# A two-layer decoder trunk on one core: the last row tile in three pieces, one weight split on VectorE, and two steps of the first mixer in another order

## The chip, the core and the metric

The kernel runs on one core of a Trainium2 chip. A core has a matrix engine (TensorE, PE in the profile; PEld is its loading of weights), a vector engine (VectorE, DVE), an engine for activation functions (ScalarE, ACT), GpSimd (POOL) and SyncE (SP), which here only issues DMA transfers. Each engine works through its own instructions in order and waits on semaphores for the others. Matrix products are written to PSUM, which has eight banks of 128 x 512 floats; all other tiles lie in SBUF.

The metric is the time of one execution on the device in microseconds. The kernel before takes 986.98 us, the median of three runs (986.97 to 987.2).

## The reference, cut to what matters

The input has 512 tokens of 1024 features. Two layers follow each other, and each is a mixer and a gated FFN, both with a residual and an RMS norm ahead; a final RMS norm ends it. All is float32.

```python
def forward(x):                       # x: 512 x 1024
    h = x
    # layer 0, even: one input projection, short gated convolution and causal pooling
    proj = rms_norm(h, norm_mix[0]) @ w_in_even          # 1024 -> 2048: b, c, v, z
    y_a = b * causal_dwconv3(c * v, conv_a)
    y_b = einsum(pool(z) - z, w_pool) * pool_scale       # windows 2, 4, 8, 16
    h = h + concat(y_a, y_b) @ w_out_even
    h = h + ffn(rms_norm(h, norm_ffn[0]), 0)
    # layer 1, odd: chunked spatial gating
    u, v = split(gelu(rms_norm(h, norm_mix[1]) @ w_in_odd))
    h = h + (u * spatial(rms_norm(v, sgu_norm))) @ w_out_odd
    h = h + ffn(rms_norm(h, norm_ffn[1]), 1)
    return rms_norm(h, final_norm)

def ffn(x, l):                        # 1024 -> 2816 -> 1024
    g = causal_dwconv3(x @ w_gate[l], conv[l]) + b[l]
    return (silu(g) * (x @ w_up[l])) @ w_down[l]
```

## The kernel before

**Products.** Each float32 operand is held as two parts of a reduced float format: `hi`, a rounded copy, and `lo`, what is left, `x - hi`. A product of two such operands is three matmuls into one PSUM bank (`mm3`, L132 to L135): hi with hi (L133), then the two mixed ones (L134, L135). Making the parts of a weight is two steps. `parts` (L125) rounds on ACT (L128) and subtracts on DVE (L129). `summed` (L116) needs no DVE: ACT writes the negated raw value (L120), a DMA issued by POOL adds it up in flight (L121), and ACT rounds `hi` (L122). Raw weights are loaded by SP into four buffers (`raw`, L109); a load starts when the last reader of its buffer is done, and SP issues its loads in order.

**Order.** The code is written against a tile framework, which places the instructions on each engine and adds the semaphores; calls wrapped in `inorder` keep their order as written. Each engine then runs its list in order, so an instruction that waits holds all that stand behind it on that engine.

**Start, `mixer0` (L333).** The input is loaded in pieces of one or two column blocks together with the matching rows of the z weight. `turn(k)` (L355) transposes block k of the input on PE into a PSUM bank (`xt_ps`, L358), rounds the weight on ACT (L366), copies the block to `h[k]` on DVE (L367), makes the scaled parts `hgh` on ACT (L369) and `hgl` on DVE (L371) from `h[k]`, the low weight part on DVE (L370), and the square for the norm on ACT. `group` (L137) runs the products: block k of the contraction against four column groups, and `ahead` (L377) calls `turn` one block before it is used (blocks 0 and 1 together). Behind the z group the weights of the pooling projection (`wpl`, L426 to L431) are loaded by SP and split, `wpl_hi` on ACT (L430) and `wpl_lo` on DVE (L431). This split stands in neither order as written, and in the built lists it comes between blocks 3 and 4 of z on DVE and on ACT. The norm's scale is applied later: `rstd_tokens` sums the squares on PE (L197, L198), and its root on ACT (L227) and four steps on DVE follow.

**FFN, `Ffn.both` (L651).** Hidden features go in pairs f, f + 1 of 128. For most pairs gate and up are computed by seven products in place of eight on halves of the operands: `s12`, `s34` and so on are sums of raw weight blocks on DVE (L668 to L675), each split into parts (L648, L649). The lower half of the raw weights (`raws[key, 1]`) is split by `summed` (L676), except in the last pair. PE runs 14 products of 12 matmuls (L639). ACT copies results out (L698) and DVE adds others onto them (L703, L708). In layer 1 the pair f = 4 is followed by the down projection of features 0 and 1 (`dn`, 48 matmuls), then by f = 6, and then by f = 8 in `seven` (L726), whose first sums on DVE, called s14 and s23, stand at L746 to L748.

**End, `ffn1` (L1123).** The last down projection takes four hidden blocks (18 to 21) for four row tiles of 128 tokens and two halves of 512 columns: eight groups of 12 matmuls, in `group8` (L1293), row tile by row tile. `done` (L1263) follows each group: DVE adds the product onto the residual `y` (L1266), ACT squares it and sums the squares along the row (L1271), DVE multiplies by the final norm's gain (L1275). After the second half the mean of squares (L1281) goes to `newton` (L223): the root on ACT (L227), its reciprocal on DVE (L228), and one Newton step (L229, L230, L1284), and DVE scales both halves (L1287), which SP stores (L1289).

Of the kernel before, what the change touches and what calls it, by code (L numbers as in the profile page):

```python
# [8 lines left out]
F32 = mybir.dt.float32  # L9
# [3 lines left out]
ALU = mybir.AluOpType  # L13
# [17 lines left out]
def tile_trunk(ctx: ExitStack, tc: tile.TileContext, x, norm_mix, norm_ffn, final_norm,  # L31
# [104 lines left out]

    def group(name, outs, ks, lhs, rhs, tail, on_done, before=None, at_end=None):  # L137
# [172 lines left out]

    def in_group(name, w, c0, lhs_is_weight, on_done, tail, chunks=None, before=None):
        if chunks is None:
# [15 lines left out]
        if lhs_is_weight:  # L328
            group(name, range(4), list(range(NK)), wt, lambda k, j: hg_k(k), tail, on_done, before)
        else:  # L330
            group(name, range(4), list(range(NK)), tokens, wt_wide, tail, on_done, before)

    def mixer0():  # L333
        nonlocal prm0
        w = w_in_even[0]
        with tc.tile_pool(name="m0", bufs=1) as mp:
# [18 lines left out]
            def turn(k):  # L355
# [3 lines left out]
                if k in raws:  # L359
# [5 lines left out]
                whi, wlo, wraw = zchunks[k]  # L365
                inorder(nc.scalar.activation(whi, wraw, AF.Copy))  # L366
                inorder(nc.vector.tensor_copy(h[k], ps))  # L367
                g = prm_mix("mix", k)
                inorder(nc.scalar.activation(hg[k][0], h[k], AF.Copy, scale=g))  # L369
                inorder(nc.vector.tensor_tensor(wlo, wraw, whi.bitcast(F32), ALU.subtract))  # L370
                inorder(nc.vector.scalar_tensor_tensor(  # L371
                    hg[k][1], h[k], g, hg[k][0].bitcast(F32), op0=ALU.mult, op1=ALU.subtract))
                norm.square(k, inorder)
                if k == 0:
                    load(6, 2)

            def ahead(k):  # L377
                for i in (0, 1) if k == 0 else (k + 1,):
                    if i < NK:
                        turn(i)  # L380

# [40 lines left out]

            in_group("z", w, 1536, True, z_done, 2, zchunks, ahead)
            prm0 = params0()
# [4 lines left out]
            wpl_lo = mp.tile([P, 4, P], F32R, name="wpl_lo")  # L429
            nc.scalar.activation(wpl_hi, wpl, AF.Copy)  # L430
            nc.vector.tensor_tensor(wpl_lo, wpl, wpl_hi.bitcast(F32), ALU.subtract)  # L431

# [9 lines left out]

            in_group("ac", w, 512, True, c_done, 4)

            cv = {}
# [43 lines left out]
    class Ffn:  # L489
# [161 lines left out]
        def both(self, f):  # L651
# [12 lines left out]
            for key in "gu":  # L664
# [458 lines left out]
    def ffn1(norm):  # L1123
        with tc.tile_pool(name="f1", bufs=1) as ap:
# [7 lines left out]
            y = [y_all[:, t, :] for t in range(NT)]  # L1132
            ssf = ap.tile([P, NT, PAD], F32, name="ssf")[:, :, :2]

# [7 lines left out]
            def before(i, j):  # L1142
                if i < 2:
                    turn_residual(j, i)

            def minus(dst, x, y_):
# [10 lines left out]
            def down(a):  # L1157
# [74 lines left out]
                yield  # L1232

            for groups, a, b in (((0, 2, 4), 0, 2), ((6, 8), 2, 6), ((10, 12), 6, 10),
                                 ((14, 16), 10, 14), ((18, 20), 14, 18), ((), 18, 22)):
# [16 lines left out]

                def lhs(ft, j):
                    ts_ = slice((j // 2) * P, (j // 2 + 1) * P)
                    return acts[ft][0][:, ts_], acts[ft][1][:, ts_]

                def rhs(ft, j):
                    c = slice((j % 2) * 512, (j % 2 + 1) * 512)
                    return ch[ft][0][:, 0, c], ch[ft][1][:, 0, c]

                yf = {}

                def done(j, ps):  # L1263
                    t, half = j // 2, j % 2
                    dst = y[t][:, half * 512 : (half + 1) * 512]
                    nc.vector.tensor_tensor(dst, ps, dst, ALU.add)  # L1266
                    if not last:
                        return
                    sq = tp.tile([P, S], F32, tag="sq", name=f"sqf{j}")
                    ss = ssf[:, t, half : half + 1]  # L1270
                    nc.scalar.activation(sq, dst, AF.Square, accum_out=ss)  # L1271
                    if half == 0:
                        yf["pair"] = ap.tile([P, 2, S], F32, tag="s", bufs=4, name=f"yf{j}")
                    yf[half] = yf["pair"][:, half, :]
                    nc.vector.tensor_tensor(yf[half], dst, fin[:, half * 512 : (half + 1) * 512],  # L1275
                                            ALU.mult)
                    if half == 0:
                        nc.vector.tensor_scalar(ss, ss, 1.0 / D, EPS, op0=ALU.mult, op1=ALU.add)
                        return
                    ms = ssf[:, t, 0:1]  # L1280
                    nc.vector.scalar_tensor_tensor(ms, ss, 1.0 / D, ms, op0=ALU.mult, op1=ALU.add)  # L1281
                    r = tp.tile([P, LINE], F32, tag="rc", name=f"rc_fin{t}")[:, :1]
                    newton(ms, 1, f"fin{t}", r)
                    nc.vector.tensor_scalar(ms, ms, 1.5, None, op0=ALU.add)  # L1284
                    for c in range(2):
                        cs = slice(c * 512, (c + 1) * 512)
                        nc.vector.tensor_scalar(y[t][:, cs], yf[c], r, ms,  # L1287
                                                op0=ALU.mult, op1=ALU.mult)
                        nc.sync.dma_start(out[t * P : (t + 1) * P, cs], y[t][:, cs])  # L1289

                group8(f"dn{a}", list(range(a, b)), lhs, rhs, 4, done)

    def group8(name, ks, lhs, rhs, tail, on_done):  # L1293
        banks = {}
        head = max(0, len(ks) - tail)
        order = [(i, j) for i in range(head) for j in range(8)]
        order += [(i, j) for j in range(8) for i in range(head, len(ks))]
        for i, j in order:
            if j not in banks:
                banks[j] = mm_bank(f"{name}_{j}") if j < 7 else aux_bank(f"{name}_{j}")  # L1300
            mm3(banks[j], lhs(ks[i], j), rhs(ks[i], j), i == 0, i == len(ks) - 1, inorder)
            if i == len(ks) - 1:
                on_done(j, banks[j])

# [34 lines left out]
```

## Time and profile before

| | |
|---|---|
| median of 3 runs | 986.98 us (986.97 to 987.2) |
| profiled execution | 988.01 us |
| its span, first to last instruction | 986.2 us |
| mean granted TensorE clock | 0.997 |
| busy PE, DVE, ACT, POOL | 973.6, 776.0, 549.5, 61.6 us |
| DMA moved, mean | 126.62 MB, 128 GB/s |

The page gives busy time of each engine over the whole span; it can't say what a stage waits for. For that the trace is asked by stretch: the timeline lists instructions with their start, their duration and, in brackets, the idle time of the engine just before them and what ended it. A row of SPq or POOLq is the issue of a DMA, not its transfer. In the chain of waits the pieces that led to the last instruction stand in order of time.

### The profile page before, as it was taken

What the parts mean: (1) busy time and instruction counts of PE and PEld (TensorE: products, weight loads), DVE (VectorE), ACT (ScalarE), POOL (GpSimd) and SP (SyncE); (2) the same over time, 40 slices, a digit from 0 to 9 for tenths busy, and PEclk for the clock granted to TensorE, in tenths of its full rate; (3) what the DMA queues carried; (4) which work ended last, traced back from release to release, by engine and by line L of the source; (5) the groups of instructions that cost most, each with busy time, mean ns of one, the idle gap of its engine ahead of it and who ended that gap; (6) DMA issues with size and microseconds to landing.
All of it is one profiled execution on the core that took longest, in us unless ns stands there. A gap on an engine that the chain in (4) does not pass through costs nothing.

```text
span 986.2 us, 14472 instructions
## 1 busy us (share of the span) xinstructions
PE 973.6 (99%) x5619; PEld 857.2 (87%) x5619; DVE 776.0 (79%) x1184; ACT 549.5 (56%) x805; POOL 61.6 (6%) x90
## 2 busy tenths in 40 slices
PE   8999999999999999999999999999999999999996
PEld 6888888898999989999888888888898989989885
DVE  6977457968776687768998686489799989898996
ACT  5623346744654646545658844568466567565752
POOL 0032000100000000000000000001000001000000
PEclk9999999999999999999999999999999999999998
DMA  6522225454445544545313412334545646556432
GB/s 227 194 104 87 87 86 128 107 150 129 108 149 149 139 140 107 151 117 195 134 57 119 150 64 87 105 99 109 137 149 153 159 138 150 149 151 171 129 86 86
DMA packets 84784, 126.62 MB, mean 128 GB/s; under 512 B 4356, under 2 KB 53740, under 8 KB 84716
## 3 DMA queue, kind: packets, MB, share of 16 engines
q1 hardware_dynamic: 76172, 100.01, 30.8%
q0 software_dynamic: 7200, 24.12, 13.1%
q10 hardware_dynamic: 1344, 1.58, 0.5%
q8 instruction: 44, 0.72, 0.3%
q14 instruction: 24, 0.20, 0.1%
HBM read 99.47 MB, written 2.10 MB: 103 GB/s over the span
## 4 chain that ended last, share of the span: by engine, by line
PE 93%; DMA 2%; DVE 2%; ACT 1%; issue 0%; SPq 0%; DVEq 0%; ACTq 0%; POOL 0%; POOLq 0%
PE d L134 4%; PE d L133 4%; PE d L135 4%; PE gu L133 2%; PE gu L135 2%; PE gu L134 2%; PE va L934 2%; PE u L133 1%; PE g L133 1%; PE oo L133 1%; PE g L134 1%; PE oo L135 1%; PE u L135 1%; PE oo L134 1%; PE g L135 1%; PE oe L134 1%
## 5 line engine op out<-in xcount | busy, mean ns | idle before, releaser
L134 PE MATMUL d<-a_lo,whi_d 128*128 128x512 f32 x176 | 68.6, 390 | 0.0
L135 PE MATMUL d<-a_hi,wlo_d 128*128 128x512 f32 x176 | 68.5, 389 | 0.0
L133 PE MATMUL d<-a_hi,whi_d 128*128 128x512 f32 x176 | 66.9, 390 | 0.0
L509 DVE SCALAR_TENSOR_TENSOR c<-rows,prm,c 128x512 f32<-128x512 f32 x88 | 64.4, 747 | 2.8 <-ACT c L507 2.8
L121 POOL DMA_DIRECT2D wlo_g<-raw_g x17 | 14.8, 871 | 414.8 <-ACT wlo_g L120 390.7
L292 DVE TENSOR_TENSOR h<-d,h 128x512 f32<-128x512 f32 x48 | 32.6, 688 | 9.4 <-PE d L135 9.3
L129 DVE TENSOR_TENSOR wlo_d<-raw_d,whi_d 128x1024 fp32r<-128x1024 f32 x22 | 26.8, 1224 | 16.5 <-ACT whi_d L128 16.5
L134 PEld LDWEIGHTS d<-a_lo,whi_d 128*128 128x128 f32 x176 | 33.0, 188 | 7.3 <-DVE a_lo L249 0.2
L133 PEld LDWEIGHTS d<-a_hi,whi_d 128*128 128x128 f32 x176 | 32.8, 188 | 7.1
L135 PEld LDWEIGHTS d<-a_hi,wlo_d 128*128 128x128 f32 x176 | 33.0, 188 | 6.8
L520 ACT ACTIVATE s<-c,prm 128x512 f32<-128x512 f32 x44 | 31.3, 717 | 12.3 <-DVE c L509 12.1
L648 ACT ACTIVATE whi_s12u<-s12u 128x1024 fp32r<-128x1024 f32 x14 | 14.8, 1059 | 39.2 <-PE d L134 33.7
L175 ACT ACTIVATE hgh<-h,prm 128x512 fp32r<-128x512 f32 x24 | 17.3, 721 | 28.4 <-DVE h L292 28.4
L648 ACT ACTIVATE whi_s12g<-s12g 128x1024 fp32r<-128x1024 f32 x14 | 14.9, 1061 | 30.6 <-DVE s12g L669 25.0
L507 ACT ACTIVATE c<-rows,prm 128x512 f32<-128x512 f32 x44 | 31.4, 719 | 1.0 <-DVE rows L703 0.4
L128 ACT ACTIVATE whi_d<-raw_d 128x1024 fp32r<-128x1024 f32 x22 | 23.2, 1056 | 14.3 <-issue 3.3
L129 DVE TENSOR_TENSOR wlo_u<-raw_u,whi_u 128x1024 fp32r<-128x1024 f32 x17 | 20.7, 1222 | 11.4 <-ACT whi_u L128 11.4
L176 DVE SCALAR_TENSOR_TENSOR hgl<-h,prm,hgh 128x512 fp32r<-128x512 f32 x24 | 17.9, 750 | 11.8 <-ACT hgh L175 11.8
L121 POOL DMA_DIRECT2D wlo_u<-raw_u x17 | 14.6, 862 | 194.9 <-ACT wlo_u L120 88.4
L133 PE MATMUL gu<-hgh,whi_u 128*128 128x512 f32 x64 | 25.4, 397 | 0.0
L133 PE MATMUL gu<-hgh,whi_g 128*128 128x512 f32 x64 | 25.4, 396 | 0.0
L133 PE MATMUL oo<-mx,whi_oo 128*128 128x512 f32 x64 | 25.2, 394 | 0.0
(1413 smaller groups left out, 3614.4 us busy)
## 6 DMA issues: line engine op xcount, KB each, us to landing
raw_g<-in_w_ffn_gate_dram SPq DMA_DIRECT2D x36, 512.0 KB, 4.0
raw_u<-in_w_ffn_up_dram SPq DMA_DIRECT2D x36, 512.0 KB, 3.7
raw_d<-in_w_ffn_down_dram SPq DMA_DIRECT2D x22, 512.0 KB, 3.7
raw_dn<-in_w_ffn_down_dram SPq DMA_DIRECT2D x22, 512.0 KB, 4.1
wlo_g<-raw_g POOLq DMA_DIRECT2D x17, 512.0 KB, 4.5
wlo_u<-raw_u POOLq DMA_DIRECT2D x17, 512.0 KB, 4.6
raw_oe<-in_w_out_even_dram SPq DMA_DIRECT2D x8, 512.0 KB, 3.5
raw_g<-in_w_ffn_gate_dram SPq DMA_DIRECT2D x16, 256.0 KB, 2.9
```

What stands on the lines that cost most here:

```text
L121: nc.gpsimd.dma_start(lo, raw, accum_op=ALU.add)
L128: nc.scalar.activation(hi, raw, AF.Copy)
L129: nc.vector.tensor_tensor(lo, raw, hi.bitcast(F32), ALU.subtract)
L133: order(nc.tensor.matmul(ps, lhs[0], rhs[0], start=start, stop=False))
L134: nc.tensor.matmul(ps, lhs[0], rhs[1], start=False, stop=False)
L135: nc.tensor.matmul(ps, lhs[1], rhs[0], start=False, stop=stop)
L292: nc.vector.tensor_tensor(h[k], ps, h[k], ALU.add)
L507: nc.scalar.activation(c, t[:, 0:S], AF.Copy, scale=prm("cf", ft))
L509: self.convolved = nc.vector.scalar_tensor_tensor(c, t[:, i : S + i], prm("cf", i * NF + ft), c, op0=ALU.mult, op1=ALU.add)
L520: nc.scalar.activation(s, c, AF.Silu, bias=self.prm("bf", ft))
L648: nc.scalar.activation(hi, src, AF.Copy)
L934: nc.tensor.matmul(ps, l, r, start=first, stop=end, skip_group_check=True)
```

## The change

There are four edits.

- **The end.** `group8` becomes `by_rows`, which keeps the order row tile by row tile, and the last row tile is cut into pieces of 512, 256 and 256 columns. `finish` takes the place of `done` for the last projection. The root now takes the sum of the last piece as its input and the mean of the earlier ones as its bias, so that it stands on ACT right behind the square; the mean is brought up to date on DVE behind it. One DVE step of the Newton step is folded into another. For the last row tile the factor `both` is made, ACT scales the last piece with it, and ACT's own queue stores it; the other two pieces are scaled on DVE and stored by SP.
- **The first tile.** For block 0 the parts are made from the PSUM bank, ahead of the copy to `h[0]`, and the weight is rounded on DVE. `group` gets `between`: the four high products of block 0 run first, then `turn(1)`, then the eight mixed products. Squares of blocks 0 and 1 stand behind both. Block 1 has an order of steps of its own (copy, high, low, then the weight).
- **The pooling split.** `wpl_hi` and `wpl_lo` are made behind the `ac` group and pinned there. The load stays where it was in SP's order. In the built lists ACT's part stands between the last `whi_ac` and the norm's root, and DVE's behind the last product copy of `ac`.
- **One weight in layer 1.** For f = 4 the lower half of the up weight is split by `parts` in place of `summed`. With it the built order of DVE and ACT for f = 6 and the first sums of f = 8 moves: on DVE the first sums of f = 6 now stand ahead of the sums that follow f = 4's products, and s14 of f = 8 ahead of the last `y` sum of `dn` and of `wlo_s12u` of f = 6.

```diff
@@ group
+            if i == 0 and between is not None:
+                l, r = lhs(ks[i], j), rhs(ks[i], j)
+                inorder(nc.tensor.matmul(banks[j], l[0], r[0], start=True, stop=False))
+                if j == outs[-1]:
+                    between()
+                    for n in outs:
+                        l, r = lhs(ks[i], n), rhs(ks[i], n)
+                        inorder(nc.tensor.matmul(banks[n], l[0], r[1], start=False, stop=False))
+                        inorder(nc.tensor.matmul(banks[n], l[1], r[0], start=False, stop=False))
+                continue
@@ turn
-                inorder(nc.scalar.activation(whi, wraw, AF.Copy))
-                inorder(nc.vector.tensor_copy(h[k], ps))
-                g = prm_mix("mix", k)
-                inorder(nc.scalar.activation(hg[k][0], h[k], AF.Copy, scale=g))
-                inorder(nc.vector.tensor_tensor(wlo, wraw, whi.bitcast(F32), ALU.subtract))
-                inorder(nc.vector.scalar_tensor_tensor(
-                    hg[k][1], h[k], g, hg[k][0].bitcast(F32), op0=ALU.mult, op1=ALU.subtract))
-                norm.square(k, inorder)
+                g, src = prm_mix("mix", k), ps if k == 0 else h[k]
...
+                def w_high():
+                    if k == 0:
+                        inorder(nc.vector.tensor_copy(whi, wraw))
+                    else:
+                        inorder(nc.scalar.activation(whi, wraw, AF.Copy))
...
+                for step in ((w_high, w_low, high, low, copy), (copy, high, low, w_high, w_low),
+                             (w_high, copy, high, w_low, low))[min(k, 2)]:
+                    step()
+                for i in ((), (0, 1))[k] if k < 2 else (k,):
+                    norm.square(i, inorder)
@@ mixer0
-            in_group("z", w, 1536, True, z_done, 2, zchunks, ahead)
+            in_group("z", w, 1536, True, z_done, 2, zchunks, ahead, lambda: turn(1))
...
-            nc.scalar.activation(wpl_hi, wpl, AF.Copy)
-            nc.vector.tensor_tensor(wpl_lo, wpl, wpl_hi.bitcast(F32), ALU.subtract)
...
             in_group("ac", w, 512, True, c_done, 4)
+            inorder(nc.scalar.activation(wpl_hi, wpl, AF.Copy))
+            inorder(nc.vector.tensor_tensor(wpl_lo, wpl, wpl_hi.bitcast(F32), ALU.subtract))
@@ both
-                hi, lo = (parts if f == NF - 2 else summed)(*raws[key, 1])
+                hi, lo = (parts if f == NF - 2 or (layer, f, key) == (1, 4, "u") else summed)(*raws[key, 1])
@@ ffn1
+            def finish(t, cs, ps):
+                dst, c, n = y[t][:, cs], cs.start, cs.stop - cs.start
+                nc.vector.tensor_tensor(dst, ps, dst, ALU.add)
...
+                ss, ms = ssf[:, t, 0:1], ssf[:, t, 1:2]
+                nc.scalar.activation(sq, dst, AF.Square, accum_out=ss)
+                if cs.stop == D:
+                    sd = work("sd", 1, f"fin{t}")
+                    nc.scalar.activation(sd, ss, AF.Sqrt, scale=1.0 / D, bias=ms)
+                nc.vector.tensor_tensor(yf[t][:, cs], dst, fin[:, cs], ALU.mult)
+                if c == 0:
+                    nc.vector.tensor_scalar(ms, ss, 1.0 / D, EPS, op0=ALU.mult, op1=ALU.add)
+                else:
+                    nc.vector.scalar_tensor_tensor(ms, ss, 1.0 / D, ms, op0=ALU.mult, op1=ALU.add)
+                if cs.stop < D:
+                    return
+                r = tp.tile([P, LINE], F32, tag="rc", name=f"rc_fin{t}")[:, :1]
+                nc.vector.reciprocal(r, sd)
+                nc.vector.scalar_tensor_tensor(ms, ms, r, r, op0=ALU.mult, op1=ALU.mult)
+                nc.vector.tensor_scalar(ms, ms, -0.5, 1.5, op0=ALU.mult, op1=ALU.add)
+                if t == NT - 1:
+                    both = ssf[:, t, 2:3]
+                    nc.vector.tensor_tensor(both, ms, r, ALU.mult)
+                for cs in (PIECES, LAST)[t == NT - 1]:
+                    rows = slice(t * P, (t + 1) * P)
+                    if cs == LAST[-1]:
+                        nc.scalar.activation(y[t][:, cs], yf[t][:, cs], AF.Copy, scale=both)
+                        nc.scalar.dma_start(out[rows, cs], y[t][:, cs])
+                    else:
+                        nc.vector.tensor_scalar(y[t][:, cs], yf[t][:, cs], r, ms,
+                                                op0=ALU.mult, op1=ALU.mult)
+                        nc.sync.dma_start(out[rows, cs], y[t][:, cs])
...
+    def by_rows(name, fts, acts, ch, pieces, on_done):
+        for t in range(NT):
+            for cs in pieces[t]:
+                whole = t < NT - 1 or cs.stop < D
+                ps = (mm_bank if whole else aux_bank)(f"{name}_{t}_{cs.start}")
+                ps = ps[:, : cs.stop - cs.start]
+                ts_ = slice(t * P, (t + 1) * P)
+                for ft in fts:
+                    mm3(ps, tuple(x[:, ts_] for x in acts[ft]),
+                        tuple(x[:, 0, cs] for x in ch[ft]), ft == fts[0], ft == fts[-1], inorder)
+                on_done(t, cs, ps)
+
+    PIECES = [slice(0, 512), slice(512, D)]
+    LAST = [slice(0, 512), slice(512, 768), slice(768, D)]
```

More of the change, by code (lines that the diff above doesn't have):

```diff
@@ L135, in mm3, with group @@
         nc.tensor.matmul(ps, lhs[1], rhs[0], start=False, stop=stop)
-    def group(name, outs, ks, lhs, rhs, tail, on_done, before=None, at_end=None):
+    def group(name, outs, ks, lhs, rhs, tail, on_done, before=None, at_end=None,
+              between=None):
         banks = {}
@@ L309, in in_parts, with in_group @@
             chunks[k + i] = hi[:, i, :], lo[:, i, :]
-    def in_group(name, w, c0, lhs_is_weight, on_done, tail, chunks=None, before=None):
+    def in_group(name, w, c0, lhs_is_weight, on_done, tail, chunks=None, before=None,
+                 between=None):
         if chunks is None:
@@ L328, in in_group @@
         if lhs_is_weight:
-            group(name, range(4), list(range(NK)), wt, lambda k, j: hg_k(k), tail, on_done, before)
+            group(name, range(4), list(range(NK)), wt, lambda k, j: hg_k(k), tail, on_done, before,
+                  between=between)
         else:
@@ L377, in ahead @@
             def ahead(k):
-                for i in (0, 1) if k == 0 else (k + 1,):
-                    if i < NK:
-                        turn(i)
+                if k == 0:
+                    turn(0)
+                elif k + 1 < NK:
+                    turn(k + 1)
             W = S + PAD
@@ L1132, in ffn1 @@
             y = [y_all[:, t, :] for t in range(NT)]
-            ssf = ap.tile([P, NT, PAD], F32, name="ssf")[:, :, :2]
+            ssf = ap.tile([P, NT, PAD], F32, name="ssf")
             def turn_residual(t, half):
@@ L1251, in ffn1 @@
                                      .rearrange("(k p) c -> p k c", p=P), 1, D, f"dn1_{ft}")
[L1253 to L1303, printed above, removed]
+                def done(t, cs, ps):
+                    dst = y[t][:, cs]
+                    nc.vector.tensor_tensor(dst, ps, dst, ALU.add)
```

16 lines of the change are left out of this document (added).

## The prediction

> **What bounds the kernel now.** I read the page first, then the waits of TensorE (PE), then the timelines around each wait, then the chain of waits at the end.
>
> ```profile
> span 986.2 us, 14472 instructions
> ...
> PE 973.6 (99%) x5619; PEld 857.2 (87%) x5619; DVE 776.0 (79%) x1184; ACT 549.5 (56%) x805; POOL 61.6 (6%) x90
> ```
>
> PE is busy for 99% of the span, and the change takes no matrix product away. So a gain can only come out of the few places where PE stands still, and out of the tail behind its last matmul. Its waits, longest of the start and of the second FFN (waited for: us in total, times, longest):
>
> ```profile
> PE xt_ps L358 <- DMA xt<-in_x_dram: 1.3, 1, 1.3
> ...
> PE u_4b L639 <- DMA wlo_u<-raw_u: 0.7, 1, 0.7
> ...
> PE z L133 <- ACT hgh L369: 0.4, 1, 0.4
> ...
> PE z L134 <- DVE hgl L371: 0.3, 1, 0.3
> ```
>
> The edits touch just these. A wait in this list is shorter than what it costs, because matmul ends are modelled past the start of the next one; I therefore price each stall by starts against the undisturbed pace.
>
> **Start: wpl's split pinned later.** Timeline of the start (start, us, engine, line, operation, idle before and its releaser):
>
> ```profile
> 10.20 0.45 PEld L358 LDWEIGHTS xt_ps<-ident,xt 128*128 128x128 f32 x4 [0.18 <-DMA xt<-in_x_dram]
> ...
> 14.39 0.40 SPq L427 DMA_DIRECT2D wpl<-in_w_pool_dram  x1
> ...
> 16.29 0.68 DVE L189 TENSOR_TENSOR ssq_m<-ssq_m,sq_m 128x512 f32<-128x512 f32 x1
> ...
> 16.69 0.60 PE L358 MATMUL xt_ps<-ident,xt 128*128 128x128 f32 x4
> ...
> 18.13 0.63 ACT L430 ACTIVATE wpl_hi<-wpl 128x512 fp32r<-128x512 f32 x1 [1.50 <-DMA wpl<-in_w_pool_dram]
> ...
> 18.79 0.69 DVE L431 TENSOR_TENSOR wpl_lo<-wpl,wpl_hi 128x512 fp32r<-128x512 f32 x1 [1.82 <-ACT wpl_hi L430]
> ...
> 19.40 0.68 DVE L367 COPY h<-xt_ps 128x512 f32<-128x512 f32 x1
> ...
> 19.90 0.60 PE L358 MATMUL xt_ps<-ident,xt 128*128 128x128 f32 x4
> ...
> 20.12 0.72 ACT L369 ACTIVATE hgh<-h,prmmix 128x512 fp32r<-128x512 f32 x1 [1.36 <-DVE h L367]
> ...
> 20.88 0.75 DVE L371 SCALAR_TENSOR_TENSOR hgl<-h,prmmix,hgh 128x512 fp32r<-128x512 f32 x1 [0.19 <-ACT hgh L369]
> ...
> 24.32 0.60 PE L358 MATMUL xt_ps<-ident,xt 128*128 128x128 f32 x4
> ...
> 32.96 0.21 ACT L227 ACTIVATE sd_m0t<-ms_m0t 128x4 f32<-128x4 f32 x1 [1.03 <-DVE ms_m0t L235]
> ...
> 64.45 1.23 DVE L129 TENSOR_TENSOR wlo_ab<-raw_ab,whi_ab 128x1024 fp32r<-128x1024 f32 x1 [1.87 <-ACT whi_ab L128]
> ```
>
> ACT stands at L430 until wpl lands at 18.13, DVE stands behind it at L431, and the copy of h[4], though its transposes (16.69 + 0.60) end at 17.29, waits in DVE's queue until 19.40. From transposes to transposes PE takes 19.90 - 16.69 = 3.21 us undisturbed and 24.32 - 19.90 = 4.42 us in this step: 1.21 us lost. With the split gone from here the copy starts at 17.33, hgh runs 18.05 to 18.77, hgl 18.81 to 19.56, and PE asks for them at 19.90 + 0.35 (the four transposes' pace) = 20.25. Slack 0.7 us, so the whole 1.21 goes; the loads behind are freed by DVE's reads, which move earlier with it. In its new place wpl_hi stands on ACT just ahead of L227, where ACT idles 1.03 us against its 0.63; wpl_lo stands on DVE ahead of the later wlo_ab, where 1.87 us idle cover its 0.69 (uncovered it would cost that, off PE's path). wpl's DMA keeps its place in SP's queue. Next late is hgl of k = 6, which by the same walk comes some 0.1 us ahead of PE: bounds 0.6 to 1.21, taken 1.21.
>
> **Start: first tile from PSUM, turn(1) between.** hgh[0] no longer waits for the copy (one COPY, 0.68, leaves the path), four high products run before x[1] is turned, and whi[0] moves from ACT to DVE. But PE's next transposes need x[2], whose weights load at 10.20 after waiting for the DMA: PE merely arrives early and stands there. In exchange squares move behind and DVE copies h[2] about 0.5 us later, still ahead of PE. whi[0] on DVE is at most another 0.68, beside PE's wait for x. Gain between 0 and the 0.18 of that row; taken 0.
>
> **Layer 1, f = 4: low part of u's lower half on DVE.** Timeline, and two pieces of the chain of waits (start, us, what):
>
> ```profile
> 681.62 0.28 PE L639 MATMUL g_4a<-hgh,whi_a 128*128 128x256 f32 x1
> ...
> 686.28 1.04 ACT L120 ACTIVATE wlo_u<-raw_u 128x1024 fp32r<-128x1024 f32 x1
> ...
> 688.30 1.23 DVE L649 TENSOR_TENSOR wlo_s34u<-s34u,whi_s34u 128x1024 fp32r<-128x1024 f32 x1 [1.61 <-ACT whi_s34u L648]
> ...
> 694.80 0.46 SPq L110 DMA_DIRECT2D raw_g<-in_w_ffn_gate_dram  x1
> ...
> 699.62 0.69 DVE L668 TENSOR_TENSOR s12g<-raw_g,raw_g 128x512 f32<-128x512 f32 x1 [3.46 <-DMA raw_g<-in_w_ffn_gate_dram]
> ...
> 702.84 0.40 PE L133 MATMUL dn<-whi_dn,a_hi 128*128 128x512 f32 x1
> ```
>
> ```profile
> 687.62 6.58 DMA wlo_u<-raw_u
> ...
> 697.14 1.44 PE g_4a L639 x12
> ```
>
> The stage is 14 products of 12 matmuls: 14 x 1.44 = 20.16, and 702.84 - 681.62 = 21.22, so 1.06 us are lost, nearly all at the summing DMA that lands at 694.2. The change drops ACT's L120 (1.04), POOL's issue and that DMA, and adds a DVE subtraction of 1.23 into a hole of 1.61 before wlo_s34u, which ACT's shorter queue also frees 1 us sooner. It ends near 687.8; PE reads it at 693.3. So 1.06 is taken, bounds 0 to 1.06.
> The raw buffer is released at 687.8 instead of 694.2, so the next loads start 4 to 6 us earlier, and DVE's order shifts: s12g of f = 6 now stands ahead of the sums that free PE's banks. Its second load follows wlo_dn (issue near 690.1) and by the rows takes 699.62 - 694.80 = 4.8, so 694.9; the sum behind it is needed at 681.62 + 11 x 1.44 = 697.5. Slack 1.9 us after its own 0.6: no stall.
>
> **Tail.** Chain and timeline behind PE's last matmul, and two groups by form (line, shape, count, then busy us and mean ns):
>
> ```profile
> 978.04 0.23 PE dn L134
> ...
> 978.53 0.70 DVE y L1266
> ```
>
> ```profile
> 979.32 0.63 ACT L1271 ACTIVATE sqf<-y 128x512 f32<-128x512 f32 x1 [1.04 <-DVE y L1266]
> ...
> 980.08 0.16 DVE L1281 SCALAR_TENSOR_TENSOR ssf<-ssf 128x1 f32<-128x1 f32 x1
> 980.27 0.20 ACT L227 ACTIVATE sd_fin<-ssf 128x1 f32<-128x1 f32 x1 [0.23 <-DVE ssf L1281]
> ...
> 981.28 1.00 DVE L1287 TENSOR_SCALAR y<-yf,rc_fin,ssf 128x512 f32<-128x512 f32 x2
> ...
> 982.32 0.35 SPq L1289 DMA_DIRECT2D out_dram<-y  x1
> ```
>
> ```profile
> L698 ACT COPY rows<-g_6a 128x256 f32<-128x256 f32 x8 | 2.8, 356 | 1.7 <-PE g_6a L639 1.7
> ...
> L719 DVE TENSOR_TENSOR s<-kept,s 128x256 f32<-128x256 f32 x14 | 5.9, 421 | 0.0
> ```
>
> Before: from y (978.53) to the last store's issue (982.32) 3.79 us. After, with 256 columns last: y 0.42, of which 0.34 until the next DVE step; the middle piece's mean must be updated before the square may overwrite its sum, 0.19, hand-over 0.04; square to its result 0.76 - (0.63 - 0.36) = 0.49; the root follows on ACT itself, 0.20 + 0.04, with no DVE step between; then the in-place mean (it must wait for the root's read) and the reciprocal behind it, 0.08; three dependent steps of 0.19 = 0.57; the scaling of 512 columns starts 0.08 later, at 2.03; 0.55 + 0.03 to SP's first issue and 0.35 to the second: 2.96. That is 0.83 less. The third piece's scaling and store go through ACT beside it. Against it, 24 matmuls at 1.44 per 12 = 2.88 for 12 x 0.23 = 2.76: +0.12. Net 0.71; ends: a loss of 0.12 (bytes of the stores, not their issue, set the end) and a gain of 1.1 (the last stores are half as large). Nearest to the rows: 0.7.
> The Trainium skill (TensorE: Matmul & The Clock Gate, "Wait — 56ns, not 53.3ns?") gives a warm matmul as its columns over 2.4 GHz plus about 2.5 ns; by it the two narrow pieces would cost 24 x 109 - 12 x 216 ns = 0.03 instead of 0.12, and the time below would be 0.1 lower. The rows decide.
> The skill (Trainium Kernel Development and Optimization, "Key Constraints") also says that all queues share the same 16 DMA engines and a second issuer saves issue time only; that would hold for the store moved to ACT, and no run here shows it yet.
>
> **Sum.** 1.21 + 0 + 1.06 + 0.7 = 2.97, about 3.0 us. The profiled execution took 988.01 (span 986.2 and 1.81 around it) and would take 985.0; it lies 1.03 above the median of 986.98, which becomes 984.0. A measurement of this kernel can tell about 0.2%, 1.97 us, from no change.
>
> **Rivals.**
> 1. The f = 4 gain fails: PE waits there for the sums queued behind s12g as it did for the DMA. For: DVE's new order. Against: 1.9 us slack. 986.98 - 1.91 = 985.1.
> 2. The start gives half: hgl of k = 6, 0.1 us ahead, comes late. 984.0 + 0.6 = 984.6.
> 3. The tail gives nothing, the stores' bytes or a slow second queue ending it: 984.0 + 0.83 = 984.8.
> 4. Slower: DVE held at s14 of f = 8. It now stands ahead of the last y sum and wlo_s12u of f = 6, and needs a load that waits for f = 6's summing DMA:
>
> ```profile
> 708.98 0.86 POOL L121 DMA_DIRECT2D wlo_g<-raw_g  x1 [20.50 <-DVE s L723]
> ...
> 713.60 0.37 SPq L110 DMA_DIRECT2D raw_u<-in_w_ffn_up_dram  x1
> ```
>
> ```profile
> 719.66 1.44 PE u_6e L639 x12
> ```
>
> PE needs wlo_s12u at 719.66 - 1.06 + 0.1 = 718.7; behind the landing come 0.6, 0.6 and 1.23. So a landing after 716.2 costs, us for us. If the summing DMA still starts at 708.98, takes 6.58 like wlo_u, and the load as long again, the landing is 722.2 and PE loses 6.0: 984.0 + 6.0 = 990.0. Against: ACT's and DVE's orders put that DMA near 704, the load near 709 and its landing near 714.
>
> **Chances.** Forecast 0.60; rival 1, 0.14; rival 2, 0.07; rival 3, 0.09; rival 4, 0.10, half of it full. Faster by over 0.2% (below 985.0): forecast and rivals 2 and 3, 0.76. Within: rival 1 and the milder half of 4, 0.19. Slower: 0.05. The range runs from 983.4 (tail at its good end and 0.18 at the first tile) to 985.9, past rival 1 by a tail without gain, and leaves rival 4 out.
>
> **What would show it.** In the changed profile: PE's z waits on hgh and hgl at k = 4 gone, the transposes of k = 4, 5 and 6 evenly 3.2 apart; PE standing longer at the transposes of x[2], still near 10.2; no wait for wlo_u and 20.2 us from g_4a to dn; DVE not idle over 1 us ahead of s14 of f = 8; 3.0 us or less from the last y to the last store's issue. Wrong if a PE wait above 0.5 stands between 680 and 725, if the distance between k = 5 and 6 stays above 4, or if the end comes as late after PE as before.

## The result, and the profile after

The changed kernel takes 985.34 us (median of 22 executions, 984.8 to 987.37) against 987.44 us (22 executions of the kernel before beside them, 986.68 to 991.6): a ratio of 0.998, 95% interval 0.9973 to 0.9986, so 1.4 to 2.7 us less. The forecast was 984.0, range 983.4 to 985.9. The profiled executions differ by more than the medians: 983.3 against 986.2 us of span, 2.9 us. Where those 2.9 us are is read first; the medians are taken up behind the experiments. One execution of the run minus_first below took 1622.36 us at a granted clock of 0.556 and is left out of its row; with it the median there is 986.48.

The page of the changed kernel, and PE's waits (waited for: us in total, times, longest):

```profile
span 983.3 us, 14491 instructions
...
PE 973.0 (99%) x5631; PEld 857.8 (87%) x5631; DVE 778.1 (79%) x1186; ACT 548.3 (56%) x806; POOL 60.9 (6%) x89
```

```profile
PE clock L56 <- DVE idle L53: 1.3, 1, 1.3
PE z L153 <- ACT hgh L394: 0.8, 1, 0.8
PE dn14e L1214 <- ACT hi L1186: 0.3, 1, 0.3
```

PE is as busy as before. Gone from its list are the waits for x, for hgh and hgl in the z products, for wlo_u at f = 4, and also the 0.5 us at f = 18 of the first layer (g_18e for rows), where no edit was made. In the list of the kernel before, that row read:

```profile
PE g_18e L639 <- DVE rows L708: 0.5, 1, 0.5
```

The same stretches in the timeline of the changed kernel:

```profile
9.96 0.60 PE L371 MATMUL xt_ps<-ident,xt 128*128 128x128 f32 x4
...
16.57 0.60 PE L371 MATMUL xt_ps<-ident,xt 128*128 128x128 f32 x4
...
19.79 0.60 PE L371 MATMUL xt_ps<-ident,xt 128*128 128x128 f32 x4
...
22.98 0.60 PE L371 MATMUL xt_ps<-ident,xt 128*128 128x128 f32 x4
...
447.51 0.39 PE L671 MATMUL g_18e<-hgh,whi_s34g 128*128 128x256 f32 x1
...
679.55 0.28 PE L671 MATMUL g_4a<-hgh,whi_a 128*128 128x256 f32 x1
...
684.53 1.22 DVE L129 TENSOR_TENSOR wlo_u<-raw_u,whi_u 128x1024 fp32r<-128x1024 f32 x1
...
699.71 0.40 PE L133 MATMUL dn<-whi_dn,a_hi 128*128 128x512 f32 x1
...
711.12 0.69 DVE L778 TENSOR_TENSOR s<-raw_u,raw_u 128x512 f32<-128x512 f32 x1
...
972.48 0.28 PE L133 MATMUL dn<-whi_dn,a_hi 128*128 128x256 f32 x1
...
975.23 0.28 PE L135 MATMUL dn<-whi_dn,a_lo 128*128 128x256 f32 x1
```

The transposes of k = 4, 5 and 6 stand 3.22 and 3.19 us apart where the second gap was 4.42. From g_4a to dn it is 20.16 us in place of 21.22. The first sum of f = 8 (s at 711.12, the s14 of rival 4) follows the one ahead of it without a gap. Before, the same g_18e read as follows:

```profile
449.53 0.39 PE L639 MATMUL g_18e<-hgh,whi_s34g 128*128 128x256 f32 x1 [0.48 <-DVE rows L708]
```

Taking the same matmul in both traces: in the z products behind the transposes of k = 5 the changed kernel is 1.33 us ahead (20.69 against 22.02), from f = 18 on 2.02 (447.51 against 449.53; 1.46 just ahead of it), at dn 3.13 (699.71 against 702.84). At PE's end it is 2.99: there 24 narrow matmuls from 972.48 take 2.75 / 23 = 0.120 us each, so 2.87 against 2.72, +0.15. The rest is the end, in the changed kernel:

```profile
975.59 0.42 DVE L1270 TENSOR_TENSOR y<-dn,y 128x256 f32<-128x256 f32 x1
...
976.65 0.29 ACT L1279 ACTIVATE sd_fin<-ssf 128x1 f32<-128x1 f32 x1
...
977.76 0.86 DVE L1300 TENSOR_SCALAR y<-yf,rc_fin,ssf 128x512 f32<-128x512 f32 x2
977.88 0.51 ACT L1297 ACTIVATE y<-yf,ssf 128x256 f32<-128x256 f32 x1 [0.94 <-DVE ssf L1293]
978.33 0.81 SPq L1302 DMA_DIRECT2D out_dram<-y  x2
978.41 0.35 ACTq L1298 DMA_DIRECT2D out_dram<-y  x1
```

SP's second issue stands at 978.33 + 0.81 - 0.35 = 978.79, 3.20 us after the last y; it was 3.79. But from there to the end of the span it is 4.51 us where it was 3.88. From the last y to the end it is 7.71 us, as before (7.67). So of the 2.9 us, 1.33 belong to the start, 0.56 to f = 18 and 1.06 to f = 4, and the end cost 0.15 + 0.04. That makes 2.76; the rest, 0.1, is small drift between these places.

### The profile page after: what moved, and what is told of

It reads as the page before. It is cut to its first block, busy times and chain, and to the rows that moved or that the text cites. A ratio compares the mean times of both kernels' runs of the same rounds, so it can differ in the third digit from the quotient of the medians.

```text
span 983.3 us, 14491 instructions
## 1 busy us (share of the span) xinstructions
PE 973.0 (99%) x5631; PEld 857.8 (87%) x5631; DVE 778.1 (79%) x1186; ACT 548.3 (56%) x806; POOL 60.9 (6%) x89
## 4 chain that ended last, share of the span: by engine, by line
PE 98%; DVE 1%; ACT 0%; issue 0%; DVEq 0%; ACTq 0%
PE d L133 4%; PE d L134 4%; PE d L135 4%; PE gu L133 3%; PE gu L135 3%; PE gu L134 3%; PE va L966 2%; PE u L133 1%; PE g L134 1%; PE g L133 1%; PE u L135 1%; PE oo L134 1%; PE oo L133 1%; PE u L134 1%; PE oe L134 1%; PE oe L133 1%
## 5 line engine op out<-in xcount | busy, mean ns | idle before, releaser
L133 PE MATMUL u<-whi_u,hgh 128*128 128x512 f32 x64 | 25.2, 394 | 0.0
```

What stands on the lines that cost most here:

```text
L133: order(nc.tensor.matmul(ps, lhs[0], rhs[0], start=start, stop=False))
```

## The experiments

Twelve kernels ran, in three groups of four; each group ran on one chip beside the kernel before (medians there 988.02, 988.29 and 988.64). Within a group medians can be compared, between groups rather the profiles.

### Each edit alone, on the kernel before

only_wpl takes the lines of the pooling split, only_first those of `group`, `in_group`, `turn` and `ahead`, only_f4 the condition in `both`, only_tail `finish`, `done` and `by_rows`; each is that part of the diff above and nothing else.

> The kernel before with the pooling split alone moved behind the ac group. Theory of the prediction: the transposes of k = 4, 5 and 6 stand 3.2 us apart, the start is 1.2 us shorter up to the transposes of k = 6, and the time 1.2 us (0.12%) lower. Rival, the start gives half because hgl of k = 6 comes late: 0.6 us. The 0.5 us wait of PE for rows at f = 18 of the first layer, which the changed kernel's profile doesn't have: if it hangs on the phase of the transfers, set by the start, it is gone here as well; if it is chance, it may stand or be gone in any profile.

> The kernel before with the first tile's new order alone. In its built order the pooling split stands on ACT one tile earlier than before, ahead of hgh of k = 3 in place of k = 4. Theory of the prediction (the new order of the first tile itself is worth 0 to 0.18 us): as the split stays unpinned, PE now waits for hgh of k = 3 until the wpl load has landed, near 18.1, plus 0.63 and 0.72, so near 19.5 where it asks at 17.0; against 1.2 us lost before, 2.4 are lost, and the time is about 1.2 us higher. Rival: the earlier reads of the first tile bring the loads forward, wpl lands a microsecond or more earlier, and the time is unchanged.

> The kernel before with the lower half of the up weight at f = 4 of the second layer split by ACT and DVE alone. Theory of the prediction: from g_4a to dn 20.2 us in place of 21.2, the time 1.06 us (0.11%) lower, and no wait of PE up to f = 8. Rival, the gain is given back by PE waiting for the sums behind s12g or for wlo_s12u of f = 6: a PE wait over 0.5 us between 680 and 725, and no gain.

> The kernel before with the new end alone. Theory of the prediction: 3.0 us from the last y to the last store's issue in place of 3.8, PE 0.12 longer, the time 0.7 us lower. Rival, read from the changed kernel's profile: the issue comes 0.6 us earlier, but the end of the span behind the last issue is longer by as much (an ACT queue to be waited for beside SP's), and PE is 0.15 longer, so the time is unchanged, within 0.2 us, in its span.

| kernel | median (lowest to highest, 12 executions) | ratio to before, 95% | span | last y to end |
|---|---|---|---|---|
| only_wpl | 989.3 (986.64 to 991.7) | 0.9996 to 1.002 | 985.3 | 7.63 |
| only_first | 988.91 (988.04 to 992.78) | 0.9996 to 1.002 | 986.6 | 7.70 |
| only_f4 | 986.53 (986.06 to 987.02) | 0.9972 to 0.9989 | 984.8 | 7.62 |
| only_tail | 987.63 (986.55 to 990.93) | 0.9986 to 1.0007 | 985.8 | 7.17 |

The profile of only_wpl has the transposes of k = 4, 5 and 6 at 17.04, 20.24 and 23.45: the 1.2 us are gone, as the walk said. Its x[2] came 0.35 later than in the profile of before (10.64 against 10.29), so 0.87 are left there. Its median, however, is not lower, where 1.2 us less was expected, and its executions spread over 5 us. The trace of only_first shows the mechanism named: the unpinned split now stands ahead of hgh of k = 3. In its timeline of ACT:

```profile
17.45 0.63 ACT L462 ACTIVATE wpl_hi<-wpl 128x512 fp32r<-128x512 f32 x1 [3.37 <-DMA wpl<-in_w_pool_dram]
17.98 0.70 ACT L394 ACTIVATE hgh<-h,prmmix 128x512 fp32r<-128x512 f32 x1
```

PE waits 1.9 us there, and the z products behind the transposes of k = 5 end up 0.8 us behind those of before. Its median is 0.9 us higher, with an interval that takes in no change. Only_f4 is the one edit that is clearly faster by itself: 20.15 us from g_4a to dn, no PE wait in the stretch, and all twelve executions within 1 us. Only_tail ends 0.5 us sooner after the last y than before, for the 0.15 us that PE takes longer. Its median, 0.4 us lower where 0.7 was expected, can't be told from that of before.

### Without f = 4's edit, and variants of the end and of f = 18, on the changed kernel

```diff
# minus_f4
-                hi, lo = (parts if f == NF - 2 or (layer, f, key) == (1, 4, "u") else summed)(*raws[key, 1])
+                hi, lo = (parts if f == NF - 2 else summed)(*raws[key, 1])
# f18
+                hi, lo = (parts if f == NF - 2 or (layer, f, key) in ((0, 18, "u"), (1, 4, "u")) else summed)(*raws[key, 1])
# tail_sp
-                        nc.scalar.dma_start(out[rows, cs], y[t][:, cs])
+                        nc.sync.dma_start(out[rows, cs], y[t][:, cs])
# tail_dve: `both` and ACT's branch left out as well
...
-                for cs in (PIECES, LAST)[t == NT - 1]:
+                for cs in PIECES:
```

> The changed kernel with f = 4's up weight split by summed again, as before. Theory: the summing DMA at f = 4 is late by a different amount in every execution, and the profiled execution of before showed it near its best. Of the kernels run so far the one without that DMA lies within 1 us (986.06 to 987.02), the others spread over 4 to 5 us (only_wpl 986.64 to 991.7). Then this kernel's fastest run lies 1.1 us above the changed kernel's 984.8, its slowest run 3 to 5 us above its fastest, and its median 1.1 to 3 us above 985.34. Rival, the spread belongs to the chip or the hour: the spread is that of the other kernels of this call, and the median 1.1 us higher.

> The changed kernel, the last piece still scaled on ACT but stored from SP's queue. In the changed kernel's profile the span ends 7.71 us after the last y, in the run of the new end alone 7.17, in the kernels with the old end 7.62 to 7.70. Theory, the wait for ACT's queue at the end costs the 0.5: the span ends 7.2 us or less after the last y, although SP's third issue comes 0.46 us later. Rival, SP's third issue sets the end: 7.6 or more. Rival, a single late packet in the changed kernel's profile by chance: 7.2, and no difference in the medians to the kernel with ACT's queue (f18, of this call).

> The changed kernel with the last tile scaled and stored in two pieces of 512 columns by DVE and SP, without the step that makes both; the matrix products still in pieces of 512, 256, 256. The scaling starts 0.19 us earlier; the first store's issue stands 2.55 us after the last y and the second 3.0. If the bytes set the end, it comes 0.1 to 0.2 us earlier than with the third piece on SP; if ACT's part helps, 0.3 later. All spans within 0.3 us of each other: the end is then not where the rest can be had.

> The changed kernel with the lower half of the up weight split by parts at f = 18 of the first layer too. There PE waited 0.2 to 0.7 us for rows in five of the six profiles so far, behind a load that the summing DMA of that weight holds up; the changed kernel's profile alone shows none. Theory, that DMA's time varies by a few tenths and the changed kernel's profile was lucky: no wait at f = 18 here, the median some 0.3 us below 985.34, and a narrower spread than 984.8 to 987.37. Rival, the changed start did away with that wait: no difference. Against both, DVE's extra 1.22 us makes another step late there: a new PE wait and a higher time.

| kernel | median (lowest to highest) | executions | span | last y to end |
|---|---|---|---|---|
| minus_f4 | 987.32 (985.71 to 989.59) | 12 | 984.4 | 7.12 |
| tail_sp | 985.53 (984.32 to 987.12) | 8 | 983.4 | 7.11 |
| tail_dve | 985.01 (984.73 to 986.38) | 5 | 982.9 | 6.81 |
| f18 | 984.46 (983.95 to 986.15) | 5 | 983.9 | 6.81 |

The lowest of minus_f4 lies 1.0 to 1.8 us above the lowest of the other three, its median 1.8 to 2.9 above their medians, and its spread is the widest of the four (3.9 us). That fits the theory that the summing DMA is late by different amounts. In the profiled executions it cost 0.9 to 1.2 us every time (20.15 or 20.16 from g_4a to dn without it, 21.09 to 21.30 with it, over five profiles); the longer waits would stand in executions that were not traced, so that part is argued from the spread, not shown.

The two ends without ACT's queue lie 0.3 us apart, 6.81 and 7.11, and f18, which has ACT's queue, also ends at 6.81. So the theory that this queue must cost 0.5 falls, and so does SP's third issue as a bound. The second queue gains nothing either: the last packet of the stores ends 5.17 us after the last y in tail_sp and in f18, and 5.02 in tail_dve. What the long ends have is told in the last section. The median of f18 is 0.55 us below that of tail_dve beside it, but with five executions each, spread over 2.2 and 1.7 us, that is not shown to be a difference.

At f = 18, PE's time from g_18a to g_18e (12 products and what is waited) is 1.44 in f18, so no wait; in the nine profiles of the kernels above and of before and after it is 1.52 to 2.32. The way is a long one: SP's load of the next raw_u needs the buffer that the summing DMA reads, DVE's s12u needs that load, and the sums that free PE's bank stand behind s12u on DVE. So the stall goes with the DMA's time: from POOL's issue to the load's issue it is 6.33 us in before, 6.54 in only_wpl (the longest stall, 0.88), 5.90 in the changed kernel (0.08). These are POOL's issue and the load that waits for the landing, in before:

```profile
435.34 0.86 POOL L121 DMA_DIRECT2D wlo_u<-raw_u  x1 [11.91 <-ACT rows L698]
...
441.67 0.37 SPq L110 DMA_DIRECT2D raw_u<-in_w_ffn_up_dram  x1
```

and in the changed kernel:

```profile
433.88 0.86 POOL L121 DMA_DIRECT2D wlo_u<-raw_u  x1 [11.90 <-ACT rows L730]
...
439.78 0.37 SPq L110 DMA_DIRECT2D raw_u<-in_w_ffn_up_dram  x1
```

The DMA's time is not all of it. With 5.83 us from issue to issue the stall is 0.09 in tail_dve, which has the new first tile, and 0.30 in minus_first (below), which has the old one. All five profiles with the old first tile and this DMA have 0.30 us or more, four of the seven with the new one have 0.12 or less. So the changed start may have a part in what was gained here, as the rival said; by what step stays open.

### Without either edit of the start, the best version, and the changed kernel again

```diff
# minus_first: group, in_group, turn and ahead as before; the split stays pinned
# minus_wpl: the split as before; the rest stays
+            nc.scalar.activation(wpl_hi, wpl, AF.Copy)
+            nc.vector.tensor_tensor(wpl_lo, wpl, wpl_hi.bitcast(F32), ALU.subtract)
...
-            inorder(nc.scalar.activation(wpl_hi, wpl, AF.Copy))
-            inorder(nc.vector.tensor_tensor(wpl_lo, wpl, wpl_hi.bitcast(F32), ALU.subtract))
# f18_dve: the edits of f18 and of tail_dve together
```

> The changed kernel with the first tile's old order (the other three edits kept). Theory of the prediction, the new order of the first tile is worth 0 to 0.18 us because PE waits for x[2] in either: x[2]'s transposes near 10.3 as in the changed kernel's kin (9.96 to 10.39), the k = 4, 5, 6 transposes 3.2 us apart, and a median within 0.3 us of after_again's. Rival, seen in only_wpl whose start gained 0.88 where the changed kernel's gained 1.33: the median is 0.4 us higher.

> The changed kernel with the pooling split unpinned again (the other three edits kept). As only_first showed, with the new first tile its ACT half stands ahead of hgh of k = 3, and PE waits there 1.9 us. Theory: the start is 1.9 to 2.1 us longer than the changed kernel's and the median that much above after_again's: the pin is worth more beside the new first tile than the 1.2 us that the profile of before shows. Rival: the lead is eaten by later slack, under 1 us.

> The changed kernel with two further edits together: parts at f = 18 of the first layer, and the last tile scaled and stored in two pieces by DVE and SP alone. Theory: f18 lay at 984.46 and tail_dve at 985.01 with f = 18 as it was, so 984.3 here, 0.5 to 0.9 us below after_again. Rival: both differences were the scatter of five runs, and it lies within 0.3 us of after_again.

> The changed kernel itself, beside the three others on the same chip. If its first profile was lucky at f = 18 and unlucky at the very end, this one shows a wait of 0.2 to 0.4 us for rows at f = 18 and ends 7.1 us after the last y, where the first showed none and 7.7. Median 985.3.

| kernel | median (lowest to highest) | executions | ratio to before, 95% | last y to end |
|---|---|---|---|---|
| minus_first | 986.08 (985.33 to 987.61) | 11 | 0.9966 to 0.9986 | 7.78 |
| minus_wpl | 988.0 (987.59 to 988.48) | 12 | 0.9985 to 1.0003 | 7.76 |
| f18_dve | 984.18 (983.96 to 985.66) | 6 | 0.9945 to 0.9971 | 6.54 |
| after_again | 985.76 (985.3 to 987.88) | 12 | 0.9967 to 0.9987 | 7.73 |

Without the pin the changed kernel is 2.24 us slower in the median, and its PE stands 1.6 us for hgh:

```profile
19.14 0.73 PE L133 MATMUL z<-hgh,whi_z 128*128 128x512 f32 x2 [1.58 <-ACT hgh L394]
```

The transposes of k = 6 stand at 25.51 there and at 23.26 in after_again, 2.25 us apart, so trace and median agree, a little above the 1.9 to 2.1 expected. Beside the new first tile the pin is worth about twice the 1.2 us that it had in the kernel before. Without the new first tile it is 0.3 us slower in the median and equal in the lowest (985.33 against 985.30), which is between the prediction's 0 to 0.18 and the rival's 0.4 and can't be told from nothing. F18_dve beats the changed kernel: five of its six executions lie between 983.96 and 984.32, where nine of after_again's twelve lie between 985.3 and 986.02. The medians are 1.58 us apart, more than the 0.5 to 0.9 expected. In the two profiles the f = 18 stall makes 0.12 of it (1.56 against 1.44) and the end 1.19 (7.73 against 6.54); what each of the two edits is worth in the executions that were not traced isn't separated. After_again has no f = 18 wait in its profile either (1.56 us from g_18a to g_18e), against what was expected, and again the long end.

**The other execution of f18_dve**, 985.66, is the profiled one, and its trace tells what it lost. PE at the start of f18_dve:

```profile
7.01 2.08 PE L153 MATMUL z<-hgh,whi_z 128*128 128x512 f32 x4 [0.78 <-ACT hgh L394]
8.89 1.05 PE L371 MATMUL xt_ps<-ident,xt 128*128 128x128 f32 x4
...
10.44 0.39 PE L158 MATMUL z<-hgl,whi_z 128*128 128x512 f32 x1
10.67 0.39 PE L159 MATMUL z<-hgh,wlo_z 128*128 128x512 f32 x1
...
11.83 0.60 PE L371 MATMUL xt_ps<-ident,xt 128*128 128x128 f32 x4
```

and of after_again:

```profile
6.88 1.21 PE L153 MATMUL z<-hgh,whi_z 128*128 128x512 f32 x4 [0.78 <-ACT hgh L394]
7.93 0.60 PE L371 MATMUL xt_ps<-ident,xt 128*128 128x128 f32 x4
...
10.22 0.60 PE L371 MATMUL xt_ps<-ident,xt 128*128 128x128 f32 x4
```

Four matmuls take 8.89 - 7.01 = 1.88 us, 0.47 each, where the other execution needs 1.05, 0.26 each; only near 10.2 the pace becomes the usual 0.23. PE ran its first products at half speed, for some 3 us longer, and the x[2] transposes came at 11.83 in place of 10.22; 1.43 us of that still stand at the transposes of k = 5 (21.48 against 20.05). The profiles of f18 (11.69) and minus_first (11.66) show the same. The granted-clock column (the third number from the end) doesn't show it; one slice of f18_dve (its length, then PE, PEld, DVE, ACT and POOL with their counts):

```profile
8.00:9.00 1.00, 1.00 (x4) 0.66 (x3) 0.34 (x1) 0.00 (x0) 0.00 (x0) 1.00 1.04 393
```

It can only be read off the pace. The Trainium skill (TensorE: Matmul & The Clock Gate, "Part 1: The HAM clock gate (the "warmup" mystery)") says that the array runs at half clock until it has been busy for one window of about 3.4 us, and that this window runs freely, so that the switch comes at another point in every run. The trace agrees with the half pace and with a switch that is about 3 us later in some executions; the window itself no run here shows.

In f18 and f18_dve the two and one executions above the others are higher by 1.3 to 2.2 us; three of them in all, two of which are these profiled ones. In after_again three of twelve stand 1.1 us and more above the rest (987.1 to 987.88), in the first runs of the changed kernel three of 22 (986.75 to 987.37). Those were not traced; that they are late switches too is likely, not shown. Minus_wpl and only_f4 have no such executions (12 each, within 0.9 and 1.0 us). Both still have the stall on the wpl load. SP issues that load between 13.86 and 14.43 in the three late starts and between 13.41 and 14.60 in the other profiles, so it does not move with PE's pace, and a start late by 1.4 us could hide in the 2.2 us of minus_wpl and all but 0.2 of it in the 1.2 us of only_f4. That fits, but no trace has both the late start and the stall, so it is argued, not shown.

## Why the prediction was right, point by point

The range and the direction held, and the forecast and its 3.0 us of gain came close to the profile's 2.9. But the agreement is luck in part, errors that cancel: the end was forecast at a gain of 0.7 and cost 0.19, so 0.9 too much, while 0.56 at f = 18, 0.12 at the first tile and 0.1 of drift were priced by no step. The range held by luck as well: 985.34 lies nearest to the 985.1 of rival 1, which did not occur.

- **The pooling split, 1.21.** Right in the profile: the gap from k = 5 to k = 6 is 3.22 and 3.19 in the changed kernel, and 3.20 and 3.21 in only_wpl, against 4.42. Rival 2 (half the gain) fell with it. In the medians the edit alone shows nothing (only_wpl, 0.9996 to 1.002); that late starts used to hide in the old stall would be a reason, but is not shown, and the spread of only_wpl is 5 us. And the price belongs to the pair of start edits, not to this one: in the changed kernel without the pin the loss is 2.24.
- **The first tile, 0.** Right: x[2]'s transposes stand at 9.96 and 10.22 in the two profiles of the changed kernel, 10.29 before, those of k = 4 at 16.57 and 16.85 against 16.69. The sign named for it was wrong, though: PE doesn't stand there for x (of the profiles with the new first tile, only tail_sp has 0.5 us of it); it stands 0.8 us for the first hgh, and its products then fill the time up to x[2]. What was not seen is that this edit, without the pin, moves the split one tile ahead and costs 0.8 us in the trace (only_first).
- **f = 4, 1.06.** Right: 21.22 became 20.16, and only_f4 has 20.15. Rival 1 (PE waits behind s12g) and rival 4 (s14 of f = 8) did not occur: no PE wait stands between 680 and 725, and DVE has no gap ahead of 711.12. In medians the edit is worth more than in the profile (988.02 to 986.53 in only_f4, 1.49 us), and it narrows the spread.
- **The end, 0.7: the failed step.** By the prediction's own sign (the end as late after PE as before) this term was wrong. The path to the last store's issue became 0.59 shorter, not 0.83: the root with its bias takes 0.29, not 0.20, the step at L1289 is 0.06 longer, and SP's second issue follows at 0.46, not 0.35. PE is 0.15 longer, not 0.12: a narrow matmul takes 0.120 us, and the estimate of 109 ns worked out from the Trainium skill (TensorE: Matmul & The Clock Gate, "Wait — 56ns, not 53.3ns?"), by which it would have been 0.03, does not hold here. And what was taken as constant, the time behind the last issue, is not: 3.88 us before, 4.51 in the changed kernel, 3.61 in f18. In the changed kernel's profiles it ate the gain. Rival 3 had the outcome but not the cause: neither the stores' bytes nor the second queue made the difference, but one packet of another kind among the last packets of the stores, 0.4 us, and a longer close behind them, 0.2 us (last section). In only_tail and minus_f4 0.4 of it remains (7.67 to 7.17 and 7.12, less 0.15).
- **ACT's store.** The other rule weighed is the Trainium skill's (Trainium Kernel Development and Optimization, "Key Constraints") that a second issuer saves issue time only. The trace agrees with it: tail_sp, with all three stores on SP, ends no later (7.11) than the same end with ACT's queue (6.81 to 7.78).
- **f = 18.** Not in the sum. The row (g_18e, 0.5) stands in the list of which the prediction shows four rows, right behind u_4b, and it was passed over; no edit touched it. It is the tail of a DMA time that varies between 5.6 and 6.5 us, and the execution profiled of before had the second longest of twelve. Whether it was that draw or the new start that took the stall away is open.
- **From profile to median.** The forecast subtracted the profile's gain from the median of three executions, 986.98; 22 give 987.44. The gain in medians is 2.1, not 3.0: the profiled execution of before lies 0.57 above its median and that of the changed kernel 0.24 below its own, which is the 0.8 between 2.9 and 2.1.
- **Two figures of the working.** 708.98 + 6.58 + 6.58 in rival 4 is 722.1, not 722.2, and the good end of the tail, 1.1, was set without a row; neither bears on the result.

## What to carry to other kernels

A stall in one profiled execution is one draw. Where it ends with a DMA that sums in flight, other executions may wait longer, and doing the step on an engine with idle time there can take away the spread with the mean (only_f4). A stall that ends at a load's landing can hide lateness ahead of it: when it is taken away, look for what was late before it (here, probably, the late rise of PE's pace). And before two edits are priced one by one, look where the second puts the instruction that the first one moves.

## What the runs showed that was not expected

- PE's half pace at the start lasts to about 7 us or less in most profiles and to about 10 us in three of fourteen, with 1.3 to 2 us in the time of f18 and f18_dve, although the kernel warms PE with 3.2 to 3.6 us of products (L56) each time.
- The end of the span after the last y takes 6.8 to 7.8 us for the same instructions. In all four profiles with 7.7 us and more and the new end, SP waits longer for the output's DMAs, here in the changed kernel:

```profile
SPq L1375 <- DMA out_dram<-y: 2.5, 3, 1.1
```

and in only_tail, with the same instructions at the end:

```profile
SPq L1343 <- DMA out_dram<-y: 1.7, 3, 1.0
```

In those four the traffic ends with two or three small packets of the stores, 0.3 us behind the others. The trace shows what stands between: one packet of 8 KB of the kind that the profile names `instruction`, on queue 14. In the changed kernel it runs from 980.74 to 981.04, and the last three packets of SP's queue start as it ends (981.04, 981.08 and 981.13). The DMA view of the changed kernel from 980.70 to 981.20 (queue and kind: packets, MB, share of the DMA engines):

```profile
DMA packets 7, 0.01 MB, mean 21 GB/s; under 512 B 4, under 2 KB 6, under 8 KB 6
...
q14 instruction: 1, 0.01, 3.9%
q1 hardware_dynamic: 6, 0.00, 1.6%
```

It starts 5.14 to 5.19 us after the last y in these four (the two profiles of the changed kernel, minus_first and minus_wpl); in the ten others none starts between 1.9 and 7.0 us after it. The last packet of the stores ends 5.54 or 5.55 us after the last y in the four, 5.16 to 5.19 in only_tail, minus_f4, f18 and tail_sp, and 5.66 to 5.68 with the old end. So the new end does bring the stores home 0.5 us sooner, and this packet takes 0.4 of it back. That it holds up the packets behind it is read from the times, in four of four; no run moved it, and why it falls there in these kernels is open. So is the close from the last packet to the end of the span, 2.21 us in the four, 1.6 to 2.0 in the other profiles.
- Only_wpl's median is 1.3 us above that of before, in the direction against its trace, with an interval that takes in no change (0.9996 to 1.002). What its untraced executions lost stays open.
